# Attention scores on all 128 rows of TensorE, with mask and maximum in one VectorE instruction

## The chip, the cores and the metric

The kernel runs on one core of one Trainium2 chip. The metric is device time in microseconds (us) of one execution, as the median of several timed runs; lower is better. Beside the timed runs there is one profiled execution, from which every row below comes. A core has TensorE (PE in the profile; its weight loads are listed apart as PEld), VectorE (DVE), ScalarE (ACT), GpSimd (POOL) and SyncE (SP), which start transfers and work side by side and wait for each other by semaphores. SBUF is the on-chip memory with 128 partitions; PSUM is the small memory in 8 banks into which TensorE writes.

## The reference

Two layers over 256 positions of width 1024. A layer is a feed-forward part, a mixer, a second feed-forward part and a gated addition. The mixer holds a sparse attention of 8 query heads over 2 key heads (64 numbers each) and a gated delta rule of 4 heads. The change is in the attention:

```python
def masked_softmax(s, mask):
    s = jnp.where(mask, s.astype(jnp.float32), NEG_INF)
    return jnp.where(mask, jax.nn.softmax(s, axis=-1), 0.0)
...
        s_c = jnp.einsum('bqhgd,bnhd->bhgqn', qb, k_cmp)
        p_cmp = masked_softmax(s_c, cmp_end[None, :] <= t[:, None])
        o_cmp = jnp.einsum('bhgqn,bnhd->bqhgd', p_cmp.astype(v_cmp.dtype), v_cmp)
...
        s_s = jnp.einsum('bqhgd,bhqnld->bhgqnl', qb, k_sel).reshape(
            b, NSA_KV_HEADS, NSA_GROUP, Q_BLOCK, n_sel * SLC_BLOCK)
        p_s = masked_softmax(s_s, m_s).reshape(b, NSA_KV_HEADS, NSA_GROUP, Q_BLOCK, n_sel, SLC_BLOCK)
        o_slc = jnp.einsum('bhgqnl,bhqnld->bqhgd', p_s.astype(v_sel.dtype), v_sel)
...
        s_w = jnp.einsum('bqhgd,bkhd->bhgqk', qb, kwb)
        p_w = masked_softmax(s_w, m_w)
        o_win = jnp.einsum('bhgqk,bkhd->bqhgd', p_w.astype(vwb.dtype), vwb)
        return gb[..., 0:1] * o_cmp + gb[..., 1:2] * o_slc + gb[..., 2:3] * o_win
```

There are three branches: over 15 compressed keys, over selected blocks of 64 keys, and over a window of 512. With 256 positions there are only 4 blocks and 16 may be selected, and no position lies outside the window, so the second and the third branch are plain causal attention, each with its own keys and values.

## The kernel before

**Tiling.** Positions stand in two tiles t of 128. Weights come from HBM through SP's queue in units of 128x2048 numbers (raw) and are split into a rounded part hi by ScalarE (L158) and a remainder lo by VectorE (L159). Every large product is three matmuls, hi by hi, hi by lo and lo by hi, so that it is nearly as exact as fp32. L273 is the helper through which all matmuls go and L277 the one for transposes, so that groups of these lines are told apart by the tiles they name: bA is the PSUM pool of the projections, bG that of the delta rule, bN that of the attention (4 banks).

**Order.** A mixer is seven generators (queries, keys, values and gates of the delta rule, the attention, the projections of weights, the output projection). The function weave resumes in a fixed ranking whichever is due; each yield says how long its result will take, and a running count of PE time sets what is due. This gives the order in which instructions are written; a scheduler then sets the order on each engine by priority and by when tiles of the pools (TAGS gives the number of buffers, BANKS the PSUM banks) come free. On an engine instructions run in that order.

**The attention.** rope (L625, L626) rotates: two products and an addition, of which GpSimd does the product with the sine and VectorE the others. nsa_prepare transposes the rotated tile into a bank and splits it into hi and lo, for the keys and for the queries. A tile then has the numbers of key head 0 on partitions 0 to 63 and those of key head 1 on 64 to 127, and all queries of four heads beside each other. compressed makes the scores over the compressed keys: one matmul writes the mask into the bank (identity by mask), then 12 of 32 columns add the scores. softmax(t, a) does the other two branches for tile t and half a of the heads. For each key head it takes a bank of 512 columns; one matmul writes the causal mask, and three matmuls per query head on 64 rows add the scores of both branches; the two key heads' matmuls alternate, on different halves of the rows. VectorE then takes the maximum of each query's row from PSUM (L1023, one instruction for 4 rows of 128 or 2 of 256), multiplies it by -1/8 (L1024), and ScalarE takes the exponent out of PSUM into SBUF tiles p, with the sum (L1027). values transposes p (L277, bN<-first,p; first holds the identity) and multiplies by the values (bN<-pT,kv). tile 0 has one pass of softmax per half, tile 1 two.

**What runs beside it.** gdn_inverse inverts the triangular matrices of the delta rule by levels (tiles ad, ab, T and TT; L816 multiplies by a level's mask on GpSimd, L832 and L836 update T and TT on VectorE). conv (L714) is the causal convolution on VectorE, gdn_scan the recurrence over 4 chunks (vb,TT is the first product of a chunk).

## Time and profile before

| what | value |
|---|---|
| median of 3 timed runs | 1193.28 us (1193.14 to 1193.42) |
| the profiled execution's own time | 1193.65 us |
| its span | 1191.9 us |
| PE busy | 1160.6 us, 97% |
| VectorE busy | 737.6 us, 62% |
| ScalarE busy | 644.4 us, 54% |
| GpSimd busy | 96.9 us, 8% |

The span runs from the first to the last instruction of the profiled execution; 1.75 us of its time lie around that. Busy time is the time in which an engine had an instruction in work. The share is a mean over the whole kernel, most of which is dense projections; the two mixers' attention lies at 240 to 364 us and at 827 to 951 us.

### The profile page before, as it was taken

To read this page: it belongs to the slowest core of one execution; us is meant where nothing else is said; L and a number is where in the kernel's file an instruction comes from. 1 tells how busy PE (TensorE), PEld (TensorE's weight loads), DVE (VectorE), ACT (ScalarE), POOL (GpSimd) and SP (SyncE) were. 2 spreads that over 40 slices of the span, in tenths; PEclk is the share of its full clock that TensorE was granted. 3 is DMA by queue.
4 is the path that set the end of the run, shared out by engine and by line. 5 is a ranking of instruction groups with operands and counts; after the bars stand their busy time and mean duration, and the time that the engine had idled before them with its cause. 6 is when DMAs were issued, how large, how long until landed. Compare 5 with 4: busy or idle time off the path is not lost.

```text
span 1191.9 us, 16067 instructions
## 1 busy us (share of the span) xinstructions
PE 1160.6 (97%) x6222; PEld 933.9 (78%) x6222; DVE 737.6 (62%) x1191; ACT 644.4 (54%) x1157; POOL 96.9 (8%) x137
## 2 busy tenths in 40 slices
PE   8999999989999999999999999999899999999996
PEld 6888888867767788888878888888676778888885
DVE  5656546887846655554675564479779365565454
ACT  7544536735766544534665454466358565454463
POOL 0000000270100000000000000004501000000011
PEclk9999999999999999999999999999999999999999
DMA  8545653422213545464554565553223144555540
GB/s 313 183 172 214 244 190 133 179 105 76 102 37 141 186 167 212 164 211 164 177 206 153 206 250 198 188 178 112 104 74 104 37 171 159 201 186 201 205 177 36
DMA packets 29292, 194.15 MB, mean 163 GB/s; under 512 B 3232, under 2 KB 3616, under 8 KB 7200
## 3 DMA queue, kind: packets, MB, share of 16 engines
q1 hardware_dynamic: 28496, 191.56, 45.0%
q10 hardware_dynamic: 720, 1.57, 0.3%
q8 instruction: 49, 0.80, 0.3%
q14 instruction: 27, 0.22, 0.1%
HBM read 192.07 MB, written 1.05 MB: 162 GB/s over the span
## 4 chain that ended last, share of the span: by engine, by line
PE 90%; DVE 4%; ACT 3%; issue 2%; POOL 1%; DMA 0%; POOLq 0%; SPq 0%; ACTq 0%; DVEq 0%
PE bA L273 50%; PE bN L273 31%; PE bG L277 4%; PE bG L273 4%; DVE lo L159 2%; PE bN L277 1%; ACT hi L158 1%; ACT p L1027 1%; POOL mn L625 0%; DMA x<-x 0%; ACT junk L925 0%; DVE mx L1023 0%; DVE ad L786 0%; DVE mn L626 0%; DVE g L450 0%
## 5 line engine op out<-in xcount | busy, mean ns | idle before, releaser
L273 PE MATMUL bA<-hi,xT 128*128 128x512 f32 (+1 forms) x1856 | 601.2, 397 | 0.9 <-DVE xT L327 0.5
L159 DVE TENSOR_TENSOR lo<-raw,hi 128x1024 fp32r<-128x1024 f32 (+2 forms) x358 | 436.8, 1225 | 213.1 <-ACT hi L158 190.7
L158 ACT ACTIVATE hi<-raw 128x1024 fp32r<-128x1024 f32 (+2 forms) x358 | 373.4, 1048 | 224.0 <-PE bN L273 118.1
L273 PEld LDWEIGHTS bA<-hi,xT 128*128 128x128 f32 x1856 | 345.3, 189 | 74.6 <-issue 4.5
L273 PE MATMUL bA<-lo,xT 128*128 128x512 f32 (+1 forms) x928 | 360.7, 390 | 0.0
L273 PEld LDWEIGHTS bA<-lo,xT 128*128 128x128 f32 x928 | 175.4, 189 | 33.9 <-issue 0.7
L273 PE MATMUL bN<-hi,n 128*128 128x512 f32 x480 | 154.2, 393 | 0.0
L273 PE MATMUL bN<-hi,g 128*128 128x512 f32 x448 | 139.9, 391 | 0.0
L273 PEld LDWEIGHTS bN<-hi,n 128*128 128x128 f32 x480 | 90.2, 188 | 18.4 <-issue 0.3
L273 PEld LDWEIGHTS bN<-hi,g 128*128 128x128 f32 x448 | 83.8, 188 | 17.1
L273 PE MATMUL bN<-lo,n 128*128 128x512 f32 x240 | 94.9, 396 | 0.0
L389 DVE SCALAR_TENSOR_TENSOR m<-bA,r,m 128x256 f32<-128x256 f32 x88 | 42.1, 479 | 79.6 <-ACT m L387 79.6
L273 PE MATMUL bN<-lo,g 128*128 128x512 f32 x224 | 87.8, 392 | 0.0
L387 ACT ACTIVATE m<-bA,r 128x256 f32<-128x256 f32 x88 | 41.5, 471 | 72.9 <-PE bA L273 69.7
L298 POOL TENSOR_SCALAR r<-ss 128x1 f32<-128x1 f32 x18 | 6.0, 333 | 827.3 <-ACT junk L291 827.3
L273 PEld LDWEIGHTS bN<-lo,n 128*128 128x128 f32 x240 | 45.1, 188 | 8.6
L273 PEld LDWEIGHTS bN<-lo,g 128*128 128x128 f32 x224 | 42.1, 188 | 8.5
L327 DVE SCALAR_TENSOR_TENSOR xT<-bG,first,xT 128x128 fp32r<-128x128 f32 x96 | 31.7, 346 | 25.5 <-ACT xT L326 25.4
L326 ACT ACTIVATE xT<-bG,first 128x128 fp32r<-128x128 f32 x96 | 32.9, 362 | 16.5 <-DVE xT L327 15.8
L395 ACT ACTIVATE g<-bG 128x256 fp32r<-128x256 f32 x48 | 18.0, 376 | 42.4 <-PE bG L277 42.2
L277 PEld LDWEIGHTS bG<-first,m 128*128 128x128 f32 x192 | 25.9, 140 | 16.9 <-DVE m L931 3.3
L277 PE MATMUL bG<-first,m 128*128 128x128 f32 x192 | 37.2, 274 | 1.8 <-DVE m L931 1.6
(219 smaller groups left out, 954.2 us busy)
## 6 DMA issues: line engine op xcount, KB each, us to landing
raw<-up SPq DMA_DIRECT2D x86, 1024.0 KB, 4.9
raw<-dn SPq DMA_DIRECT2D x44, 1024.0 KB, 4.9
raw<-win SPq DMA_DIRECT2D x24, 1024.0 KB, 4.8
raw<-wout SPq DMA_DIRECT2D x8, 1024.0 KB, 4.8
raw<-gate SPq DMA_DIRECT2D x8, 1024.0 KB, 4.8
cw<-cw SPq DMA_DIRECT2D x8, 512.0 KB, 8.1
raw<-up SPq DMA_DIRECT2D x4, 512.0 KB, 7.0
raw<-proj SPq DMA_DIRECT2D x2, 1024.0 KB, 4.7
```

Of the source, the lines that this page charges most:

```text
L158: nc.scalar.activation(hi[:, s:f], raw[:, a + s:a + f], AF.Copy)
L159: nc.vector.tensor_tensor(lo[:, s:f], raw[:, a + s:a + f], hi[:, s:f].bitcast(F32), op=OP.subtract)
L273: self.nc.tensor.matmul(out, lhsT, rhs, start=start, stop=stop, skip_group_check=part)
L277: self.nc.tensor.transpose(out, x, self.ident[:n, :n])
L298: nc.gpsimd.tensor_scalar(r, self.ss[:, 0:1], self.ss[:, 1:2], EPS, op0=OP.add, op1=OP.add)
L326: nc.scalar.activation(hi[h][:, i, cs], b[:, i, :], AF.Copy, scale=g)
L327: nc.vector.scalar_tensor_tensor(lo[h][:, i, cs], b[:, i, :], g, hi[h][:, i, cs].bitcast(F32), op0=OP.mult, op1=OP.subtract)
L387: nc.scalar.activation(s, bs[t][:, :256], AF.Silu, scale=r[t])
L389: nc.vector.scalar_tensor_tensor(h, bs[t][:, 256:], r[t], s, op0=OP.mult, op1=OP.mult)
L395: nc.scalar.activation(hh[c // 2][o], b, AF.Copy)
L1027: nc.scalar.activation(p[kv][:, i + j, br], sc[kv][:, j, br], AF.Exp, scale=0.125, bias=m[:, i + j, br:br + 1], accum_out=sm[kv][:, i + j, ...
```

## The change

The two parts of a query, hi and lo, are stacked on the partitions, and the keys are doubled so that they stand on both halves. A product over 128 rows with the keys' hi then gives hi by hi plus lo by hi, and one with the keys' lo gives hi by lo plus lo by lo: two matmuls in place of three. For key head 0 the query's hi is on partitions 0 to 63 and its lo on 64 to 127; for key head 1 the other way round, since after the transpose its numbers stand on the upper half.

- rope, called with twice, writes each rotated key twice beside itself; nsa_keys transposes 128 columns per key head and branch, four transposes per tile in place of two, and splits 128x512 numbers in place of 128x256.
- nsa_queries makes for each tile t a tile nq of 4 heads x 2 key heads x 128; hi and lo of each key head are written by two instructions of ScalarE and two of VectorE on 64 partitions.
- In compressed the mask matmul goes; 8 matmuls of 32 columns (hi beside lo) take the place of 12, and VectorE adds mask, lo part and hi part in two instructions. The small key matmul of compress becomes one in place of two, its weights stand twice in the packed constants (w2), and two GpSimd fills go.
- In softmax the mask matmuls go. VectorE's tensor_tensor_reduce adds the mask (from the packed constants, now 256 wide: zeros, then the triangle), writes the masked scores to p in SBUF and their maximum to mx, in one call for each row of 128 or 256. In the order of instructions each call is two, "ISA p,mx" and "ISA mx". ScalarE's exponent now reads and writes p in SBUF.
- The pool n has 9 buffers in place of 8, the pool n2 (2 buffers) is gone; the ple part's two tiles move from n2 to mn. Three casts of identity and masks at the start go.

```diff
@@ rope
-    def rope(self, z, t, nh):
+    def rope(self, z, t, nh, twice=False):
...
+        if twice:
+            w = self.tile("mn", [128, nh, 2, 64])
+            nc.vector.tensor_tensor(w, *(a[:, :, None, :].to_broadcast([128, nh, 2, 64]) for a in (o, u)), op=OP.add)
+            return w
         nc.vector.tensor_tensor(o, o, u, op=OP.add)
         return o
@@ compress
-        for kv in range(2):
-            self.mm(kb[kv * 64:kv * 64 + 64], w2[0], hT[:, 0, kv, :NCMP])
+        self.mm(kb, w2[0], hT[:, 0])
...
-        for p in range(2):
-            nc.gpsimd.memset(kcm[p].rearrange("p a n -> p (a n)").bitcast(F32), 0.0)
-        for kv, R in enumerate(self.HALF):
-            hi, lo = (p[R, kv, :NCMP] for p in kcm)
-            nc.vector.tensor_copy(hi, kb[R])
-            nc.vector.tensor_tensor(lo, kb[R], hi.bitcast(F32), op=OP.subtract)
+        nc.vector.tensor_copy(kcm[:, :, 0], kb)
+        nc.vector.tensor_tensor(kcm[:, :, 1], kb, kcm[:, :, 0].bitcast(F32), op=OP.subtract)
@@ in place of nsa_prepare
+    def nsa_keys(self, g, z):
...
+        hi, lo = (self.tile("n", [128, 2, 2, S], F32R) for _ in range(2))
+        for t in range(NT):
+            src = self.rope(z(t).rearrange("p (h d) -> p h d", h=4), t, 4, True)
+            yield 2.0
...
+            b = self.bank("N", [128, 2, 2, 128])
+            for br in range(2):
+                for kv in range(2):
+                    h = 2 * br + kv
+                    self.tr(b[:, kv, br], src[:, h].rearrange("p a d -> p (a d)"))
+            ts = slice(t * 128, (t + 1) * 128)
+            nc.scalar.activation(hi[:, :, :, ts], b, AF.Copy)
+            nc.vector.tensor_tensor(lo[:, :, :, ts], b, hi[:, :, :, ts].bitcast(F32), op=OP.subtract)
...
+    def nsa_queries(self, g, z):
...
+            q = self.tile("n", [128, 4, 2, 128], F32R, name="nq")
+            for kv, (R, O) in enumerate(((A, B), (B, A))):
+                nc.scalar.activation(q[R, :, kv], b[R], AF.Copy)
+                nc.vector.tensor_tensor(q[O, :, kv], b[R], q[R, :, kv].bitcast(F32), op=OP.subtract)
@@ compressed
-            cs = self.bank("N", [128, 4, 2, 16])
-            self.mm(cs.rearrange("p i k n -> p (i k) n"), self.idr, self.maskc[:, t, None, :].to_broadcast([128, 8, 16]), True, False, True)
+            cs = self.bank("N", [128, 4, 2, 2, 16])
             for i in range(4):
-                scores(cs[:, i], t, slice(0, 128), i, lambda b: kcm[b])
+                for kv in range(2):
+                    self.mm(cs[:, i, kv], q[t][:, i, kv], kcm[:, kv])
...
+            nc.vector.tensor_tensor(pf, cs[:, :, 1], self.c[:, None, C_CM + t * 16:C_CM + t * 16 + 16]
+                                    .to_broadcast([128, 8, 16]), op=OP.add)
+            nc.vector.tensor_tensor(pf, cs[:, :, 0], pf, op=OP.add)
@@ softmax
-                    self.mm(sc[kv][:, :, :, t * 128:t * 128 + 128].rearrange("p j b k -> p (j b) k"), self.idr,
-                            self.mask[:, None, :].to_broadcast([128, 2 * nb, 128]), True, False, True)
-                for j in range(nb):
-                    for n, (x, y) in enumerate(((0, 0), (0, 1), (1, 0))):
-                        for kv, R in enumerate(HALF):
-                            self.mm(sc[kv][:, j], q[x][R, a * 2 + i + j, cols(t)], k[y][R, :, :nk * 128],
-                                    False, n == 2, True)
-                for kv in range(2):
+                    for j in range(nb):
+                        for part in range(2):
+                            self.mm(sc[kv][:, j], q[t][:, a * 2 + i + j, kv], k[part][:, kv, :, :nk * 128],
+                                    not part, bool(part), True)
                     m = mx[kv]
-                    nc.vector.tensor_reduce(m[:, s], sc[kv], axis=AX.X, op=OP.max)
+                    for j in range(nb):
+                        for br in range(2):
+                            nc.vector.tensor_tensor_reduce(p[kv][:, i + j, br], sc[kv][:, j, br],
+                                                           self.c[:, C_TRI + 128 - t * 128:C_TRI + 256], 1.0, -3e38,
+                                                           op0=OP.add, op1=OP.max,
+                                                           accum_out=m[:, i + j, br:br + 1])
...
-                            nc.scalar.activation(p[kv][:, i + j, br], sc[kv][:, j, br], AF.Exp, scale=0.125,
+                            nc.scalar.activation(p[kv][:, i + j, br], p[kv][:, i + j, br], AF.Exp, scale=0.125,
```

The change also moves instructions, in three places that matter. The first is GpSimd's order in the first mixer where the queries are rotated: L625 (L619 after) is rope's product with the sine for the keys (kv) and the queries (q), L816 (L809 after) the level masks of the triangular inverse. Before:

```order
L795 TENSOR_TENSOR ke<-y,eg 128x512
L816 TENSOR_TENSOR ab<-ad,cst 128x256 x5
L625 TENSOR_TENSOR mn<-q,cst 128x8x32 x2
L816 TENSOR_TENSOR ab<-ad,cst 128x256 x2
L625 TENSOR_TENSOR mn<-q,cst 128x8x32 x2
L816 TENSOR_TENSOR ab<-ad,cst 128x256 x5
```

After:

```order
L788 TENSOR_TENSOR ke<-y,eg 128x512
L809 TENSOR_TENSOR ab<-ad,cst 128x256 x7
L619 TENSOR_TENSOR mn<-q,cst 128x8x32 x2
L809 TENSOR_TENSOR ab<-ad,cst 128x256
L619 TENSOR_TENSOR mn<-q,cst 128x8x32 x2
L809 TENSOR_TENSOR ab<-ad,cst 128x256 x4
```

Seven level masks stand ahead of the first half of the queries now, and five did before.

The second is VectorE's order in the first mixer at tile 0's compressed scores (tiles pc, m and s) and first softmax. Before:

```order
L981 TENSOR_REDUCE m_2508<-bN 128x8
L982 TENSOR_TENSOR pc<-bN,m_2508 128x128
L985 TENSOR_REDUCE s_2512<-pc 128x8
L986 RECIPROCAL s_2512<-s_2512 128x8
L987 SCALAR_TENSOR_TENSOR s_2512<-s_2512,cst,sg 128x8
L989 TENSOR_TENSOR pc<-pc,s_2512 128x128
L1023 TENSOR_REDUCE mx<-bN 128x4 x2
L1024 TENSOR_SCALAR mx<-mx 128x4 x2
```

After:

```order
L990 TENSOR_TENSOR pc<-bN,cst 128x128
L826 STREAM_TRANSPOSE TT<-T 128x256
L992 TENSOR_TENSOR pc<-bN,pc 128x128
L1034 ISA p,mx<-bN,cst 128x128
L1034 ISA mx 128x1
L994 TENSOR_REDUCE m_2500<-pc 128x8
L1034 ISA p,mx<-bN,cst 128x128
L1034 ISA mx 128x1
L995 TENSOR_TENSOR pc<-pc,m_2500 128x128
L1034 ISA p,mx<-bN,cst 128x128
L1034 ISA mx 128x1
```

In place of two reductions stand eight pairs, each with a row of its own, and the compressed scores' chain is spread between them.

The third is PE's order in the first mixer where the last values of tile 1 meet the scan of the delta rule. Before:

```order
L277 MATMUL bN<-first,p 128x128 x4
L277 MATMUL bG<-first,y 128x128 x2
L273 MATMUL bG<-vb,TT 64x128 x2
L277 MATMUL bN<-first,p 128x128 x4
L273 MATMUL bG<-vb,TT 64x128 x2
L277 MATMUL bN<-first,p 128x128 x3
L273 MATMUL bN<-pT,kv 64x256 x4
L277 MATMUL bN<-first,p 128x128
L273 MATMUL bG<-y,ao 64x128 x4
L277 MATMUL bN<-first,p 128x128 x7
```

After:

```order
L271 MATMUL bG<-first,y 128x128 x2
L267 MATMUL bN<-pT,kv 64x256 x3
L271 MATMUL bN<-first,p 128x128 x5
L271 MATMUL bG<-first,y 128x128 x4
L271 MATMUL bN<-first,p 128x128
L267 MATMUL bG<-vb,TT 64x128 x4
L271 MATMUL bN<-first,p 128x128 x4
L267 MATMUL bG<-y,ao 64x128 x4
```

Before, the scan's first product (bG<-vb,TT) stands among the first transposes of tile 1's weights; now most of these transposes and of their products with the values stand ahead of it.

## Rows read from the trace of the kernel before

**Rows 1.** The page: its head, part 1 (busy time), part 4 (chain).

```profile
span 1191.9 us, 16067 instructions
...
PE 1160.6 (97%) x6222; PEld 933.9 (78%) x6222; DVE 737.6 (62%) x1191; ACT 644.4 (54%) x1157; POOL 96.9 (8%) x137
...
PE 90%; DVE 4%; ACT 3%; issue 2%; POOL 1%; DMA 0%; POOLq 0%; SPq 0%; ACTq 0%; DVEq 0%
```

**Rows 2.** Windows: us, busy PE, PEld, DVE, ACT, POOL; clock; DMA; GB/s.

```profile
240.40:266.90 26.50, 21.70 (x205) 17.26 (x203) 22.18 (x38) 9.42 (x15) 19.86 (x20) 0.94 0.26 97
266.90:290.20 23.30, 23.23 (x290) 18.50 (x290) 16.23 (x40) 11.51 (x32) 2.92 (x3) 1.00 0.25 93
290.20:331.90 41.70, 40.24 (x221) 29.69 (x220) 35.96 (x87) 30.72 (x89) 3.70 (x6) 1.00 0.25 87
331.90:363.50 31.60, 30.44 (x196) 21.94 (x195) 14.16 (x36) 17.39 (x44) 2.43 (x4) 1.00 0.09 30
```

**Rows 3.** Chain of waits: start, length in us, what; pieces on TensorE.

```profile
140.22 49.44 PE bN L273 x218
...
275.77 1.55 PE bN L273 x13
...
290.83 0.44 PE bN L277 x4
...
296.99 0.58 PE bN L273 x4
298.00 1.13 PE bN L273 x8
...
303.43 1.01 PE bN L273 x4
...
329.99 1.29 PE bN L273 x4
```

**Rows 4.** Timeline of TensorE: start, length, instructions, [idle before them].

```profile
260.11 1.15 PE L273 MATMUL bG<-T,ab 64*64 64x64 f32 x32 [2.53 <-DVE T L832]
...
277.96 0.63 PE L273 MATMUL bN<-mask,idr 128*128 128x512 f32 x2
278.52 0.97 PE L273 MATMUL bN<-n,n 64*128 64x256 f32 x12
279.43 1.15 PE L273 MATMUL bG<-T,ab 64*64 64x64 f32 x32
```

**Rows 5.** Timeline of VectorE, same columns.

```profile
242.31 1.25 DVE L626 TENSOR_TENSOR mn<-mn 128x256 f32<-128x256 f32 x1
...
256.43 1.21 DVE L626 TENSOR_TENSOR mn<-mn 128x512 f32<-128x512 f32 x1 [1.31 <-POOL mn L625]
...
259.56 0.74 DVE L832 TENSOR_TENSOR T<-T,bG 128x256 f32<-128x256 f32 x2
...
280.11 1.28 DVE L1023 TENSOR_REDUCE mx<-bN 128x4 f32<-128x512 f32 x2
...
296.06 2.03 DVE L714 SCALAR_TENSOR_TENSOR y<-bG,small,y 128x255 f32<-128x255 f32 x5
```

**Rows 6.** Single lines: shortest/median/longest in ns, first and last start, forms.

```profile
L775 DVE SCALAR_TENSOR_TENSOR dc<-bG,gc,cst x16: 339/339/342, 237.2 to 827.3; 128x128 f32<-128x128 f32 x16
...
L714 DVE SCALAR_TENSOR_TENSOR y<-bG,small,y x72: 465/474/483, 212.9 to 913.8; 128x255 f32<-128x255 f32 x24, 128x254 f32<-128x254 f32 x24, 128x253 f32<-128x253 f32 x24
```

**Rows 7.** Timeline of ScalarE: an exponent with its accumulator read.

```profile
281.76 0.19 ACT L1027 ACTIVATION_READ_ACCUMULATOR p<-bN,mx 128x1 f32 x1
281.86 0.36 ACT L1027 ACTIVATE p<-bN,mx 128x128 f32<-128x128 f32 x1
```

**Rows 8.** Timeline of GpSimd at the queries' rotation.

```profile
254.01 2.39 POOL L625 TENSOR_TENSOR mn<-q,cst 128x256 f32<-128x256 f32 x2
256.36 1.87 POOL L816 TENSOR_TENSOR ab<-ad,cst 128x256 f32<-128x256 f32 x2
```

**Rows 9.** Windows again, two microseconds after the idle stretch; columns as above.

```profile
262.00:264.00 2.00, 2.00 (x11) 1.16 (x11) 0.70 (x1) 0.00 (x0) 1.29 (x2) 0.50 0.00 0
```

More of the change, by code (lines that the diff above doesn't have):

```diff
@@ L72, in constants @@
     c[:, C_SIN:C_SIN + 128] = sin.reshape(2, 128, 64).transpose(1, 0, 2).reshape(128, 128)
-    c[:, C_TRI:C_TRI + 128] = np.where(q <= r, 0.0, NEG)
+    c[:, C_TRI + 128:C_TRI + 256] = np.where(q <= r, 0.0, NEG)
     for t in range(NT):
@@ L236, in constants @@
         nc.gpsimd.memset(self.half, 0.5)
-        self.idr = self.cp.tile([128, 128], F32R, name="idr")
-        nc.gpsimd.tensor_copy(self.idr, self.ident)
-        self.mask = self.cp.tile([128, 128], F32R, name="mask")
-        nc.gpsimd.tensor_copy(self.mask, self.c[:, C_TRI:C_TRI + 128])
-        self.maskc = self.cp.tile([128, NT, 16], F32R, name="maskc")
-        nc.gpsimd.tensor_copy(self.maskc.rearrange("p t n -> p (t n)"), self.c[:, C_CM:C_CM + 32])
     def units(self, stages):
@@ L405, in ple @@
         nc.scalar.dma_start(praw, self.a["pT"][l].rearrange("p (k t) -> p k t", k=2))
-        ph, pl = self.tile("n2", [128, 2, S], F32R), self.tile("n2", [128, 2, S], F32R)
+        ph, pl = self.tile("mn", [128, 2, S], F32R), self.tile("mn", [128, 2, S], F32R)
         nc.scalar.activation(ph, praw, AF.Copy)
@@ L548, in attention @@
             yield from until(z, "kv", 1.0)
-            yield from self.nsa_prepare(g, "nk", lambda t: z["kv"][:, t, :256], 4, "n2")
+            yield from self.nsa_keys(g, lambda t: z["kv"][:, t, :256])
             yield from until(z, "q", 1.0)
-            yield from self.nsa_prepare(g, "nq", lambda t: z["q"][:, t], 8, "n")
+            yield from self.nsa_queries(g, lambda t: z["q"][:, t])
             yield from self.nsa(g, z["kv"])
@@ L634, in compress @@
         vc = [head(t, 160) for t in range(NT)]
-        kcm = [self.tp.tile([128, 2, 16], F32R, tag=f"kcm{i}", bufs=1, name=f"kcm{i}") for i in range(2)]
+        kcm = self.tp.tile([128, 2, 2, 16], F32R, tag="kcm", bufs=1, name="kcm")
         vcm = self.tp.tile([128, 8, 64], F32, tag="vcm", bufs=1, name="vcm")
@@ L672, in compress @@
         yield 0.6
-        w2 = [self.sm[:, l, S_W2 + 64 * i:S_W2 + 64 * i + 64] for i in range(2)]
-        kb = self.bank("N", [128, NCMP])
+        w2 = self.sm[:, l, S_W2:S_W2 + 128], self.sm[:, l, S_W2 + 128:S_W2 + 192]
+        kb = self.bank("N", [128, 2, 16])
         vb = self.bank("N", [128, 64])
-        for kv in range(2):
-            self.mm(kb[kv * 64:kv * 64 + 64], w2[0], hT[:, 0, kv, :NCMP])
+        self.mm(kb, w2[0], hT[:, 0])
         hv = self.tile("mn", [128, 4, 2, 16])
@@ L942, in gdn_finish @@
         g["gdn"] = get
[L944 removed]
+    def nsa_keys(self, g, z):
         nc = self.nc
[L947 to L948 removed]
+        hi, lo = (self.tile("n", [128, 2, 2, S], F32R) for _ in range(2))
         for t in range(NT):
[L950 removed]
+            src = self.rope(z(t).rearrange("p (h d) -> p h d", h=4), t, 4, True)
             yield 2.0
[L952 to L958 removed]
+            b = self.bank("N", [128, 2, 2, 128])
[6 more added lines that the diff above has]
+            nc.vector.tensor_tensor(lo[:, :, :, ts], b, hi[:, :, :, ts].bitcast(F32), op=OP.subtract)
+        g["nk"] = hi, lo
+        yield 1.0
+    def nsa_queries(self, g, z):
+        nc = self.nc
+        A, B = self.HALF
+        g["nq"] = []
+        for t in range(NT):
+            src = self.rope(z(t).rearrange("p (h d) -> p h d", h=8), t, 8)
+            yield 2.0
+            b = self.bank("N", [128, 4, 128])
+            for f in range(4):
+                self.tr(b[:, f], src[:, 2 * f:2 * f + 2].rearrange("p h d -> p (h d)"))
+            q = self.tile("n", [128, 4, 2, 128], F32R, name="nq")
+            for kv, (R, O) in enumerate(((A, B), (B, A))):
+                nc.scalar.activation(q[R, :, kv], b[R], AF.Copy)
+                nc.vector.tensor_tensor(q[O, :, kv], b[R], q[R, :, kv].bitcast(F32), op=OP.subtract)
+            g["nq"].append(q)
         yield 1.0
@@ L1006, in softmax @@
             nb = 2 // nk
-            ps[t, a] = p = [self.tile("n", [128, 2, 2, nk * 128], name="p") for _ in HALF]
+            p = [self.tile("n", [128, nb, 2, 2, nk * 128], name="p") for _ in range(nk)]
+            ps[t, a] = p = [p[kv][:, 0] if t else p[0][:, kv] for kv in range(2)]
             mx, sm = ([self.tp.tile([128, 2, 2], F32, tag=n, bufs=4, name=n) for _ in HALF] for n in ("mx", "smx"))
```

28 lines of the change are left out of this document (8 added, 20 removed).

## The prediction

> **What bounds the kernel now.** I read the page first, then busy time by stretch, then the chain of waits, then the timelines of single engines. The page gives a span of 1191.9 us with TensorE busy for 97% of it and VectorE for 62%, and the chain that ended last runs over TensorE for 90% [rows 1]. So a matmul taken away should count, unless the place it is taken from waits for something else. The change lies in the two mixers alone, and their attention occupies 123 us of each. The table by stretch [rows 2] cuts these 123 us into four, and a different thing limits each. In the first (keys and queries rotated, the triangular inverse begun) TensorE is busy for 21.7 of 26.5 us and VectorE for 22.2: PE waits. In the second (inverse, first scores) PE is full, 23.2 of 23.3, and VectorE has 7.1 us to spare. In the third (the other scores, the convolutions of q and v) PE is busy for 40.2 of 41.7 and VectorE for 36.0: two engines near full at once. In the fourth (the scan, values, start of the output projection) PE is busy for 30.4 of 31.6 and VectorE for only 14.2. The second mixer runs the same program some 587 us later, so I work out one mixer and double it.
>
> **The change, part by part.** All durations are from the profiled execution of 1193.65 us, which is 0.37 us above the median of the three timed runs.
>
> TensorE, compressed scores: a mask matmul and 12 score matmuls of 32 columns take 1.55 us [rows 3]. That is about 0.11 us for a matmul of 32 columns, as much as a 128-column transpose takes (four in 0.44 [rows 3]), so a narrow one costs its weight load. Eight remain: 0.9 us. Twice per mixer: -1.2.
>
> TensorE, first tile: two mask matmuls and 12 of 256 columns run from 277.96 to the next group's start at 279.43, 1.47 us [rows 4]. Eight matmuls of 256 columns on 128 rows replace them. A 512-column matmul on 128 rows takes 0.227 us (218 of them in 49.44 us [rows 3]), so half the columns are 0.114 and the eight 0.91. Twice: -1.1.
>
> TensorE, second tile: four iterations. Where both heads' banks were free, masks and three pairs took 1.13 us together [rows 3]. Where they were not, each head ran by itself, in 1.01 to 1.29 [rows 3], as long as the pair. Two iterations went the first way (one of them cut by a transpose group; I take it as equal) and two the second: 2 x 1.13 + 4 x 1.1 = 6.7 us. After: 16 x 0.227 = 3.6. -3.0.
>
> TensorE, keys: four transposes more at 0.11, +0.4; one small matmul of the compression less, -0.1. Sum for TensorE: -5.0 us per mixer, -10 in all, if nothing else ended later.
>
> VectorE, maximum: a 128x512 maximum steps at 0.60 us (two in 1.28 less the tail [rows 5]), 12 per mixer, 7.2 us. In their place stand 16 instructions of 128 elements, 16 of 256, and behind each a read of its accumulator; the trace has neither. The nearest rows for the first are a two-tensor instruction from PSUM with a scalar pointer: 0.339 us for 128 elements and 0.474 for 255 [rows 6]; five of the latter back to back take 2.03 [rows 5], a step of 0.39, so 0.26 for the short one. For the read, ScalarE's accumulator read is nearest: 0.19 us long, with the next instruction 0.10 after it began [rows 7]. I take 0.10, so pairs of 0.36 and 0.49: 13.6 us, +6.4. The ends are 0.20 and 0.33 with nothing for the read (+1.3, no scalar to fetch, by the ratio of 0.60 for 512) and full durations with a full read, 0.53 and 0.66 (+11.8).
>
> VectorE, other: two more operations of about 0.25 per compressed tile, +1.0; four half-height subtractions for the queries instead of two full ones, which cost as much each, +1.3; keys twice as wide, +0.3 each for two subtractions and two rotations, +1.2. ScalarE gets two query copies more and reads scores from SBUF; the third stretch has it at 30.7 of 41.7 [rows 2], so I charge nothing, and at most the 1.2 us of the copies if that cover went. Removed fills and casts on GpSimd lie in the first microsecond or in idle time: nothing.
>
> Now by stretch.
>
> First: +1.7. GpSimd's order moves: two multiplications by level masks, which now stood behind the rotation of the queries' first half, come ahead of it. The two took 1.87 us, the rotation before them 2.39 [rows 8]. VectorE's addition for these queries already waited 1.31 us for GpSimd at 256.43 [rows 5], and behind it in VectorE's queue stand a key subtraction, a weight subtraction and the update T at 259.56, for which PE sat idle 2.53 us [rows 4, 5]. Add 0.9 for the wider keys ahead, take off 0.2 that the weights gain from a quiet GpSimd: T comes about 2.6 late. PE gets three more projection matmuls into that gap (0.7), and does fewer later while its clock is at half (granted 0.50 in 262 to 264 [rows 9]), so I give back 0.9. The ends: +0.8 if only the wider keys count, +4 if PE idles long enough that the clock falls a second time.
>
> [...]
>
> Second: -1.7, TensorE's 0.6 and 1.1. VectorE gains 1.3 (queries), 0.5 and 16 x 0.36 - 4 x 0.60 = 3.4, 5.2 us, under its 7.1 idle [rows 2].
>
> Third: +0.5. PE loses 3.6 (0.6 and 3.0), but VectorE gains 16 x 0.49 - 8 x 0.60 + 0.5 = 3.5 against 5.7 idle, and PE must take in work from the fourth stretch: the chain of conv, maximum and exponent then ends on VectorE, slightly later.
>
> Fourth: -2.0. In PE's order 18 transposes and 8 value matmuls of the second tile now stand ahead of the scan's first product. At 0.11 and 0.29 (two in 0.58 [rows 3]) they are 4.3 us; about half should come out of the stretch, the rest was cover for the scan's hops between engines.
>
> Sum: +1.7 - 1.7 + 0.5 - 2.0 = -1.5 per mixer, -3.0 in all: 1193.65 - 3.0 = 1190.65, and 0.37 less as a median, **1190.3 us**.
>
> **The rivals.** (1) TensorE's whole saving arrives: 2 x 5.0 less, 1183.3. For it: 90% of the chain. Against: the first stretch, where PE waits, and the third, where VectorE is at 86%. (2) VectorE becomes the bound of stretches two and three, slower: pairs at 0.53 and 0.66. The third gains 16 x 0.17 = 2.7 and the second, with 7.9 against 7.1 idle, 1.4, so the mixer is at +2.6 and the run at 1198.5. It decides from about 0.06 us more per pair than I took, where the gain is used up. For it: two accumulators' worth of instructions that no row prices, in a queue that projection weights share. Against: VectorE waits for exponents at the first tile now. (3) The first stretch costs +3.2, since PE's clock falls again after the longer wait: everything cancels, 1193.3. (4) Pairs of 64-row matmuls already fill the array, and stacking buys nothing but the masks: first tile -0.2 each, second tile 0 (3 x 0.227 + 2 x 0.114 = 0.91 before, 0.91 after). Then the first stretch is +1.7, the second -1.0, the third +0.5 and the fourth -1.0 (less room on PE): +0.2 per mixer, and the run at 1193.65 + 0.4 - 0.37 = 1193.7. Against it: pairs broken at half the iterations, where a head alone took as long as two.
>
> [...]
>
> **How the numbers follow.** Forecast 0.45, whole saving 0.10, VectorE bound 0.27, clock 0.10, pairs 0.08. A difference under 0.2% (2.4 us: 1190.9 to 1195.7) is about what a measurement of this kernel can't tell from none. The forecast's own range is 1187 to 1193 (the cheap end of the accumulator below, half of the fourth stretch's gain lost above), and I put two thirds of it under 1190.9. Faster: 0.30 of the forecast and the whole saving, 0.40. Slower: the VectorE case and half of the clock case, 0.32. Between: 0.15 of the forecast, the pairs and the other half of the clock case, 0.28. Since cases of both signs hold much, the whole range has to reach past 1198.5 above and near the whole saving below: 1184 to 1200.
>
> **What would show it.** The score matmuls' groups at 0.23 us per 512 columns with no head running alone; the accumulator read's step on VectorE; VectorE's addition for the queries waiting longer for GpSimd and PE idle near 260 for 3 to 4 us; VectorE near 95% in the third stretch; a fourth stretch under 30 us. It is wrong if pairs cost over 0.55 us, or if PE idles in the third stretch waiting for weights or maxima.

## The result and the profile after

The changed kernel takes **1181.8 us** as a median of four runs (1180.72 to 1182.93) against 1193.35 for the kernel before in the same comparison: a ratio of 0.9899, with a 95% interval of 0.9881 to 0.9916. It is faster by 11.55 us. The forecast was 1190.3, with a range of 1184 to 1200: the sign was right, the size was a quarter of what came, and the time lies below the range. The four runs fall in two groups, 1180.7 and 1181.3 us with a mean granted clock of 0.998, and 1182.3 and 1182.9 with 0.994.

The profiled execution took 1180.72 us. Its page answers to [rows 1]: TensorE is as full as before, and VectorE has barely more to do (742.2 us, 737.6 before).

```profile
span 1178.9 us, 16017 instructions
...
PE 1146.9 (97%) x6150; PEld 929.2 (79%) x6150; DVE 742.2 (63%) x1303; ACT 646.9 (55%) x1161; POOL 95.9 (8%) x130
...
PE 89%; DVE 3%; ACT 3%; issue 2%; POOL 2%; DMA 0%; POOLq 0%; SPq 0%; ACTq 0%
```

The four stretches of the first mixer. They are cut at the same instructions as [rows 2] (the key casts, the fourth product with T, the first transposes of gq, the transposes just ahead of the scan), but the fourth ends here at the first matmul that reads g (bN<-hi,g), 3 us behind the end in [rows 2]. Columns: length in us, busy time of PE, PEld, DVE, ACT, POOL, then granted clock, DMA share, GB/s.

```profile
240.27:264.87 24.60, 19.95 (x205) 16.05 (x204) 19.67 (x34) 9.53 (x15) 18.82 (x20) 1.00 0.28 102
264.87:286.70 21.83, 21.72 (x277) 18.32 (x278) 19.26 (x66) 13.07 (x34) 3.85 (x3) 1.00 0.24 81
286.70:330.60 43.90, 41.92 (x235) 31.35 (x234) 39.39 (x133) 35.60 (x101) 3.45 (x4) 1.00 0.29 106
330.60:359.97 29.37, 28.22 (x173) 21.30 (x172) 13.55 (x28) 13.82 (x32) 2.51 (x4) 1.00 0.10 36
```

The fourth in the kernel before, to the same matmul:

```profile
331.90:366.37 34.47, 33.31 (x208) 24.28 (x207) 14.98 (x38) 19.14 (x46) 2.43 (x4) 1.00 0.13 48
```

First 26.5 to 24.6, second 23.3 to 21.8, third 41.7 to 43.9, fourth 34.5 to 29.4: 6.3 us less for the mixer. The third stretch is longer because it takes in work that the fourth no longer has (235 recorded PE instructions in place of 221, and 173 in place of 208 in the fourth). Counted by dense matmuls (the products of hi and lo parts in projections and feed-forward, 4272 on record in either kernel), the piece from the 900th to the 1300th, which holds the first mixer, takes 171.3 us in place of 177.6, and the piece from the 3000th to the 3400th, with the second mixer, 168.4 in place of 174.6: 6.3 and 6.2 us less.

Now the terms. On TensorE, the first tile's eight score matmuls, and two of the second tile's (the step is from one start to the next):

```profile
275.35 1.10 PE L267 MATMUL bN<-n,nq 128*128 128x256 f32 x8
276.38 1.15 PE L267 MATMUL bG<-T,ab 64*64 64x64 f32 x32
...
292.40 0.62 PE L267 MATMUL bN<-n,nq 128*128 128x512 f32 x2
292.86 0.39 PE L267 MATMUL bA<-hi,xT 128*128 128x512 f32 x1
```

Eight in 1.03 us (0.91 was taken), two in 0.46, so 0.23 each, as taken.

On VectorE, the new pairs for 128 elements, and one for 256 between convolutions:

```profile
286.00 0.28 DVE L1034 CUSTOM_DVE_ANT_0 p<-bN,cst 128x128 f32<-128x128 f32 x1
286.21 0.08 DVE L1034 DVE_READ_ACCUMULATOR2_ANT mx<- 128x1 f32 x1
286.21 0.29 DVE L1034 CUSTOM_DVE_ANT_0 p<-bN,cst 128x128 f32<-128x128 f32 x1
...
316.10 0.42 DVE L1034 CUSTOM_DVE_ANT_0 p<-bN,cst 128x256 f32<-128x256 f32 x1
316.44 0.08 DVE L1034 DVE_READ_ACCUMULATOR2_ANT mx<- 128x1 f32 x1
316.44 0.48 DVE L707 SCALAR_TENSOR_TENSOR y<-bG,small,y 128x254 f32<-128x254 f32 x1
```

The next instruction starts when the accumulator read starts, so the read costs nothing: a pair steps at **0.21 us** for 128 elements and **0.34** for 256, where the forecast had taken 0.36 and 0.49. That is 16 x 0.21 + 16 x 0.34 = 8.8 us per mixer in place of 13.6.

In the first stretch: GpSimd's product with the sine for the queries, VectorE's addition that waits for it, a weight subtraction, the update T, and TensorE behind it. These answer to [rows 4, 5, 8].

```profile
255.38 1.42 POOL L619 TENSOR_TENSOR mn<-q,cst 128x256 f32<-128x256 f32 x2
```

```profile
256.84 0.69 DVE L624 TENSOR_TENSOR mn<-mn 128x512 f32<-128x512 f32 x1 [2.02 <-POOL mn L619]
...
258.05 1.22 DVE L159 TENSOR_TENSOR lo<-raw,hi 128x1024 fp32r<-128x1024 f32 x1
259.18 0.74 DVE L825 TENSOR_TENSOR T<-T,bG 128x256 f32<-128x256 f32 x2
```

```profile
259.74 1.15 PE L267 MATMUL bG<-T,ab 64*64 64x64 f32 x32 [2.45 <-DVE T L825]
```

The addition waits 2.02 us for GpSimd where it had waited 1.31, as foreseen. But T is not late: from the key casts to T it is 18.9 us, and before it was 19.1.

### The profile page after: what moved, and what is told of

Same layout as the page of the kernel before. It is cut to its first block, busy times and chain, and to the rows that moved or that the text cites. A ratio compares the mean times of both kernels' runs of the same rounds, so it can differ in the third digit from the quotient of the medians.

```text
span 1178.9 us, 16017 instructions
## 1 busy us (share of the span) xinstructions
PE 1146.9 (97%) x6150; PEld 929.2 (79%) x6150; DVE 742.2 (63%) x1303; ACT 646.9 (55%) x1161; POOL 95.9 (8%) x130
## 3 DMA queue, kind: packets, MB, share of 16 engines
q1 hardware_dynamic: 28496, 191.69, 44.6%
## 4 chain that ended last, share of the span: by engine, by line
PE 89%; DVE 3%; ACT 3%; issue 2%; POOL 2%; DMA 0%; POOLq 0%; SPq 0%; ACTq 0%
PE bA L267 49%; PE bN L267 31%; PE bG L271 4%; PE bG L267 4%; ACT hi L158 1%; PE bN L271 1%; DVE lo L159 1%; POOL mn L619 1%; POOL ab L809 1%; DMA x<-x 0%; ACT junk L918 0%; ACT p L1041 0%; ACT junk L734 0%; DVE ad L779 0%; DVE y L707 0%
## 5 line engine op out<-in xcount | busy, mean ns | idle before, releaser
L267 PE MATMUL bN<-hi,n 128*128 128x512 f32 x448 | 143.6, 392 | 0.0
L267 PEld LDWEIGHTS bN<-hi,n 128*128 128x128 f32 x448 | 84.0, 188 | 16.8 <-issue 0.3
L267 PE MATMUL bN<-lo,n 128*128 128x512 f32 x224 | 89.1, 398 | 0.0
L267 PEld LDWEIGHTS bN<-lo,n 128*128 128x128 f32 x224 | 42.1, 188 | 8.6 <-issue 0.8
```

What stands on the lines that cost most here:

```text
L267: self.nc.tensor.matmul(out, lhsT, rhs, start=start, stop=stop, skip_group_check=part)
```

## The experiments

All medians stand beside 1193.2 to 1193.8 for the kernel before in the same comparisons, and 1181.8 for the changed kernel. The "third stretch" is here from the first transposes of gq to the scan's first product, first and second mixer; the last column is the piece between the third and the fourth product with T, in which the granted clock was 0.75 in both mixers of before, 0.72 in the first of e1_stack and 1.00 in both of the changed kernel.

| kernel | median, us | third stretch | third to fourth T |
|---|---|---|---|
| before | 1193.35 | 42.4 / 42.4 | 6.8 / 6.9 |
| changed | 1181.8 | 44.6 / 44.6 | 5.1 / 5.1 |
| e1_stack | 1183.55 | 44.5 / 44.5 | 6.1 / 5.1 |
| e2_ttr | 1189.6 | 43.9 / 43.9 | 5.3 / 6.8 |
| e3_vec2 | 1199.36 | 51.0 / 52.3 | 6.1 / 5.1 |
| e4_rope_dve | 1177.98 | 46.0 / 45.8 | 6.2 / 6.2 |
| e5_vec_half | 1191.47 | 50.2 / 50.3 | 6.1 / 6.1 |
| e6_vec_t0 | 1185.6 | 45.7 / 47.7 | 5.1 / 6.1 |
| e7_noneg | 1178.36 | 42.8 / 42.8 | 5.1 / 5.1 |
| e8_both | 1173.93 | 42.8 / 42.8 | 6.2 / 6.2 |
| e9_offchain | 1186.74 | 48.9 / 47.8 | 5.1 / 5.1 |
| e10_before_rope | 1188.27 | 42.4 / 42.4 | 5.3 / 5.3 |
| e11_pool | 1181.92 | 43.4 / 43.4 | 6.2 / 6.2 |

**Which half of the change gives the gain.** e1_stack keeps the stacked scores and takes mask and maximum as before:

```diff
+                    self.mm(sc[kv][:, :, :, t * 128:t * 128 + 128].rearrange("p j b k -> p (j b) k"), self.idr,
+                            self.mask[:, None, :].to_broadcast([128, 2 * nb, 128]), True, False, True)
...
-                            nc.vector.tensor_tensor_reduce(p[kv][:, i + j, br], sc[kv][:, j, br],
...
+                    nc.vector.tensor_reduce(m[:, s], sc[kv], axis=AX.X, op=OP.max)
```

> The changed kernel with the causal masks as matmuls and the maximum as one reduction again, and the exponent out of PSUM; scores stay stacked on 128 rows, the compressed scores as changed. Theory A (the time follows TensorE's work, whatever VectorE does): the 12 mask matmuls per mixer come back, 4 of 512 columns at 0.227 us and 8 of 256 at 0.114, 1.8 us per mixer, so 1181.8 + 3.6 = 1185.4 us. Theory B (pairs of 64-row matmuls filled the array already, and the masks were the gain): stacking alone keeps little more than the compressed scores' 1.2 per mixer, 1193.3 - 2.4 = 1191 us.

Measured 1183.55 us (ratio 0.9917, 0.9892 to 0.9942). Theory B falls: stacking with the compressed scores alone brings nearly 10 of the 11.5 us (in the profiled executions some 2.5 of them stand in the last column of the table, which is the clock; more on it below). The masks cost 1.75 us, half of what A expects from TensorE. The maximum as one reduction is 7.2 us of VectorE per mixer against 8.8 for the pairs, and TensorE idles less for it in the third stretch (44.40 - 42.76 = 1.6 us against 2.4).

e2_ttr is the other half: the 64-row scores of before, mask and maximum on VectorE.

```diff
-                    self.mm(sc[kv][:, :, :, t * 128:t * 128 + 128].rearrange("p j b k -> p (j b) k"), self.idr,
-                            self.mask[:, None, :].to_broadcast([128, 2 * nb, 128]), True, False, True)
...
-                    nc.vector.tensor_reduce(m[:, s], sc[kv], axis=AX.X, op=OP.max)
+                            nc.vector.tensor_tensor_reduce(p[kv][:, i + j, br], sc[kv][:, j, br],
```

> The kernel before, its scores on 64 rows as they were, with the mask added and the maximum taken by VectorE and the exponent from SBUF; compressed scores as before. Theory A with pairs that stay broken at half of the iterations: only the mask matmuls go, 1193.3 - 3.6 = 1189.7 us. Theory C (a PSUM bank comes free when VectorE has read it and no longer waits for four exponents, so both heads run together): the second tile's four iterations take 3 x 0.227 = 0.68 us each in place of 6.7 in all, -4.0, and the first tile loses 1.0, so 5 us per mixer and 1183.3 us: nearly the whole gain without any stacking.

Measured 1189.6 us (ratio 0.9961, 0.9946 to 0.9976), theory A to the tenth; C falls, the pairs stay broken. That it fits to the tenth is in part luck: in the profiled executions 1.6 of the 4.2 us stand in the last column (6.8 / 6.9 to 5.3 / 6.8), and A knows nothing of the clock. The timeline of TensorE in e2_ttr shows both kinds (start, length; six matmuls are both heads, three one head):

```profile
300.34 0.96 PE L271 MATMUL bN<-n,n 64*128 64x512 f32 x3
...
318.98 0.96 PE L271 MATMUL bN<-n,n 64*128 64x512 f32 x6
319.87 0.50 PE L271 MATMUL bA<-hi,xT 128*128 128x512 f32 x1
```

Six matmuls of both heads take as long as three of one. The six take 0.89 us to the next group, and four stacked ones 4 x 0.23 = 0.92. So the rival on pairs had its fact right and its conclusion wrong: a full pair is as good as stacking, but in the first pass over tile 1 all four heads ran alone. Stacked, the two matmuls of one head by itself step at 0.23 us each (at 292.40 us above), so that a head needs no other beside it. Which wait keeps the banks apart was not tried.

**What VectorE's price is worth.** e3_vec2 gives every pair twice, e5_vec_half those of key head 0 (range(2 - kv)), e6_vec_t0 those of tile 0 (range(2 - t)).

```diff
+                            for _ in range(2):
                                 nc.vector.tensor_tensor_reduce(p[kv][:, i + j, br], sc[kv][:, j, br],
```

> The changed kernel with each mask-and-maximum instruction given twice, the second with the same result. A pair steps at 0.21 us for 128 elements and about 0.29 for 256 in the trace, so VectorE has 8 us more per mixer: 3.4 in the stretch of the first scores, where it is idle for 2.6 of 21.8 us, and 4.6 in the stretch after it, where it is idle for 4.5 of 44.6. Theory A (VectorE has room, the prediction's price was simply too dear): 0.5 to 2 us per mixer, 1183 to 1186 us. Theory D (VectorE is as near to being the bound as the prediction had it, and was only cheaper than thought): the pairs now cost 0.42 and 0.58, between the forecast's price and that of its VectorE rival, and the gain is gone: 1190 to 1194 us.

Measured 1199.36 us (ratio 1.0046, 1.0024 to 1.0067): slower than the kernel before, past both theories. The expectation had read 0.29 us for 256 elements, and the step is 0.34: VectorE has 8.8 us more per mixer, and 8.8 us per mixer is what it costs.

> The changed kernel with the mask-and-maximum instructions of key head 0 given twice and those of key head 1 once. A pair steps at 0.21 us for 128 elements and 0.34 for 256, so VectorE has 4.4 us more per mixer and 13.2 for all pairs: the price that the prediction took for the changed kernel (13.6). Theory D1 (in these stretches VectorE's time arrives in the end one for one, as twice the price cost 17.5 us for 17.6 us of work): 1181.8 + 8.8 = 1190.6 us, so that the prediction's error was the price and nothing else. Theory D2 (there is room first, as the idle shares say, 2.6 and 4.5 us per mixer, and only what goes beyond it costs): 1182 to 1185 us, and at its own price the prediction would still have been too slow.

Measured 1191.47 us (ratio 0.998, 0.9961 to 0.9999), as D1 has it. At the price that the prediction took for the pairs, the kernel lands 1.2 us from its forecast. In the profiled executions about 2 of the 9.7 us stand in the last column (5.1 to 6.1 in both mixers), ahead of a mixer's first pair.

> The changed kernel with the mask-and-maximum instructions given twice for tile 0 alone, 16 x 0.21 = 3.4 us more per mixer, nearly all in the stretch of the first scores. If VectorE counts everywhere one for one: 1181.8 + 6.7 = 1188.5 us. If it counts in the third stretch alone (in the run with all of them twice TensorE stood still at 318 to 332 us, in the third stretch): 1182 to 1184 us.

Measured 1185.6 us (ratio 0.9936, 0.9912 to 0.996), between the two. So "one for one" is not a law here, and the traces say what it is made of. First the third stretch of the changed kernel (first mixer), then of e5_vec_half, then of e6_vec_t0 in its first and second mixer, columns as above:

```profile
286.70:331.30 44.60, 42.19 (x236) 31.39 (x234) 40.09 (x135) 35.60 (x101) 3.45 (x4) 1.00 0.29 104
```

```profile
286.50:336.70 50.20, 46.21 (x239) 33.17 (x237) 44.18 (x161) 35.63 (x101) 3.45 (x4) 0.90 0.27 94
```

```profile
286.50:332.20 45.70, 41.89 (x238) 31.24 (x236) 41.96 (x156) 36.51 (x106) 3.45 (x4) 1.00 0.29 104
868.80:916.50 47.70, 44.38 (x239) 32.75 (x237) 42.06 (x156) 36.67 (x106) 3.45 (x4) 0.93 0.27 99
```

In e5_vec_half the stretch is 5.6 us longer. TensorE's idle time accounts for 1.6 of it (3.99 in place of 2.41); the other 4.0 is the same work at a lower granted clock, 0.90 in place of 1.00. In e6_vec_t0 the same code ran once at 1.00 and once at 0.93, and the second took 2.0 us longer. What TensorE did before the clock fell in e5_vec_half (timeline of TensorE, then windows of 2 us):

```profile
323.03 0.63 PE L271 MATMUL bN<-first,p 128*128 128x128 f32 x4 [1.47 <-DVE mx L1035]
324.74 0.79 PE L267 MATMUL bN<-pT,kv 128*64 128x256 f32 x4 [1.08 <-ACT pT L1061]
```

```profile
322.00:324.00 2.00, 0.63 (x4) 0.42 (x4) 2.00 (x7) 2.00 (x5) 0.00 (x0) 1.00 0.51 78
324.00:326.00 2.00, 1.26 (x7) 0.75 (x8) 1.99 (x8) 2.00 (x8) 0.00 (x0) 0.78 0.92 385
326.00:328.00 2.00, 1.31 (x5) 0.46 (x3) 1.78 (x7) 1.26 (x3) 0.00 (x0) 0.50 0.15 61
328.00:330.00 2.00, 2.00 (x6) 0.61 (x5) 2.00 (x9) 0.00 (x0) 0.00 (x0) 0.50 0.00 0
```

VectorE is full, the last maxima of tile 1 come late, TensorE has run out of dense work to put in between, waits 1.47 and 1.08 us in a row, and then runs at a granted clock of 0.50 until about 335 us (0.50 from 326 to 334, 0.66 from 334 to 336, 1.00 behind it). In the changed kernel the same place has one wait of 1.73 us for pT, and the clock stays at 1.00. In e4_rope_dve (below) it has one of 1.74, and there the clock fell: 46.0 us in place of 44.6. First the changed kernel, then e4_rope_dve:

```profile
324.01 0.65 PE L267 MATMUL bN<-pT,kv 128*64 128x256 f32 x4 [1.73 <-ACT pT L1060]
```

```profile
321.41 0.65 PE L267 MATMUL bN<-pT,kv 128*64 128x256 f32 x4 [1.74 <-ACT pT L1060]
284.10:330.10 46.00, 43.71 (x236) 32.04 (x234) 40.04 (x135) 35.66 (x101) 3.45 (x4) 0.96 0.28 101
```

So a later maximum makes TensorE wait, and whether the clock falls behind such a wait is not settled by its length here.

e9_offchain puts about the same amount of work beside the chain:

```diff
                         nc.vector.tensor_scalar(p[kv][:, i, br], p[kv][:, i, br], m[:, i, br:br + 1], None, op0=OP.mult)
+                        if not kv:
+                            nc.vector.tensor_reduce(self.tiny(1, "jk"), p[kv][:, i, br], axis=AX.X, op=OP.max)
```

> The changed kernel with as much extra VectorE work as the run with key head 0's instructions twice, but off the attention's chain: after each scaling of p for key head 0 a maximum of the scaled row into a scrap tile that nobody reads (128 or 256 elements, about 0.2 and 0.35 us each, 4.4 us per mixer). Theory G (VectorE's queue as such is short, whoever's work is in it): about 1190 us, as with the work in the chain (1191.5). Theory H (it is the chain from scores over maximum and exponent to the freed bank that grows longer; work beside it finds room): 1182 to 1185 us.

Measured 1186.74 us (ratio 0.9941, 0.9922 to 0.9961), between G and H. Its third stretch is 48.9 us at a clock of 0.90, with 3.3 us idle, 2.74 of them in the wait for pT:

```profile
287.10:336.00 48.90, 45.64 (x237) 33.12 (x234) 43.28 (x145) 35.67 (x101) 3.46 (x4) 0.90 0.28 97
324.95 1.12 PE L267 MATMUL bN<-pT,kv 128*64 128x256 f32 x4 [2.74 <-ACT pT L1062]
```

So work that nobody waits for costs too: conversions and maxima stand behind it in VectorE's order, and of the 4.3 us more in this stretch 0.9 are idle time of TensorE and 3.4 the lower clock. In the chain it costs about twice as much in all (a part of it stands behind the last convolution of the stretch, so that 2.5 us per mixer is rather a lower bound for work beside the chain).

**Less on VectorE.** e7_noneg multiplies the keys by -1/8 where they are split, and the negation of the maximum goes:

```diff
-            nc.scalar.activation(hi[:, :, :, ts], b, AF.Copy)
+            nc.scalar.activation(hi[:, :, :, ts], b, AF.Copy, scale=-0.125)
...
-                                                           op0=OP.add, op1=OP.max,
+                                                           op0=OP.add, op1=OP.min,
...
-                    nc.vector.tensor_scalar(m[:, s], m[:, s], -0.125, None, op0=OP.mult)
```

> The changed kernel with the keys multiplied by -1/8 where they are split, so that VectorE takes a minimum, which is the exponent's bias as it is: the 12 multiplications of the maximum per mixer go (0.08 to 0.16 us each, 1.0 to 1.9 per mixer), and no engine gets an instruction more. Theory D1 (VectorE one for one, in both directions): 2 to 4 us less, 1178 to 1180 us. Theory D2 (there is room on VectorE, so less of it buys nothing): 1181 to 1182 us.

Measured 1178.36 us (ratio 0.987, 0.9842 to 0.9898): D1. The changed kernel's 2.4 us of idle TensorE in the third stretch are gone:

```profile
287.60:330.40 42.80, 42.65 (x237) 31.23 (x235) 38.78 (x115) 33.87 (x93) 3.45 (x4) 1.00 0.28 100
```

That bounds it as well: with 0.15 us left idle, more relief on VectorE has nothing to give in this stretch.

**The first stretch.** e4_rope_dve lets VectorE do the queries' product with the sine; e10_before_rope does the same to the kernel before.

```diff
-            nc.gpsimd.tensor_tensor(u[:, :, h:h + 32], z[:, :, 32 - h:64 - h], tab(C_SIN + h, 32), op=OP.mult)
+            (nc.vector if nh == 8 else nc.gpsimd).tensor_tensor(u[:, :, h:h + 32], z[:, :, 32 - h:64 - h], tab(C_SIN + h, 32), op=OP.mult)
```

> The changed kernel with the queries' products with the sine on VectorE in place of GpSimd (two instructions of 256 elements per tile of positions). Theory E (in the first stretch the update T waits behind an addition that waits 2.0 us for GpSimd, twice, and TensorE idles 4.7 us of 25.5 for that): 1.5 to 2 us per mixer less, about 1178 us. Theory F (VectorE is the chain there, and 1.4 us more work on it comes on top): 1181.8 to 1184 us.

Measured 1177.98 us (ratio 0.9868, 0.9838 to 0.9898): theory E. TensorE's wait before the third product with T, 2.45 us, becomes 0.17 and 0.45:

```profile
256.24 0.68 PE L267 MATMUL bG<-T,ab 64*64 64x64 f32 x16 [0.17 <-DVE T L825]
...
258.04 0.68 PE L267 MATMUL bG<-T,ab 64*64 64x64 f32 x16 [0.45 <-DVE T L825]
```

> The kernel before, with the queries' products with the sine on VectorE in place of GpSimd, as tried on the changed kernel, where it gave 3.8 us. If the change left the first stretch as it was: the same 3.8 here, 1193.3 - 3.8 = 1189.5 us. If the change had made the wait for GpSimd there 1.7 us per mixer longer, as the prediction's sum has it, the kernel before has that much less to gain: 0.4, 1192.9 us.

Measured 1188.27 us (ratio 0.9962, 0.9947 to 0.9976), 5.4 us less than the 1193.7 beside it, more than either expectation. The total doesn't settle it, because in the profiled executions 3 us are the clock (the last column, 6.8 to 5.3 in both mixers). The piece between the second and the third product with T does: VectorE's rotation takes it from 7.4 to 5.8 us in the kernel before, and from 7.9 to 4.9 in the changed one. So the wait for GpSimd did become dearer with the change, by about 1.4 us per mixer of what can be won back, near the prediction's 1.7. But the way up to the second product, from the transposes of gc, became 0.7 us shorter (17.3 to 16.6), so that with the half microsecond more behind it (7.4 to 7.9) the way to T did not grow.

**The clock in the first stretch.** The last column of the table holds the same matmuls in the kernel before, e2_ttr and e10_before_rope (76 to 78 on record): 6.8 us or 5.3. In the versions of the changed kernel it is 6.1 or 5.1 (73 on record). (In e4, e8 and e11 T's order is another.) The windows of e2_ttr, first and second mixer:

```profile
260.40:265.70 5.30, 5.30 (x77) 4.08 (x78) 4.06 (x9) 1.37 (x3) 2.77 (x3) 1.00 0.01 3
844.50:851.30 6.80, 6.80 (x76) 5.16 (x76) 4.07 (x9) 1.34 (x3) 2.78 (x3) 0.75 0.01 4
```

One execution, the same code, the same wait before it (2.40 and 2.41 us): at a granted clock of 0.75 the piece takes 1.5 us more. The profiled execution of before had it in both mixers [rows 9], the changed one in neither. So about 3 of the 13 us between the two profiled executions are this. Whether it strikes after a wait of 2.4 us differs between passes through the same code; after the 0.9 us that e10_before_rope leaves of the wait it struck in neither mixer. Why it strikes in one pass and not in the next stays open.

**Versions that beat both.** e8_both joins e4_rope_dve and e7_noneg.

> The keys' multiplication by -1/8 together with the queries' rotation on VectorE. If both act in their own stretches the gains add: 1178.0 less what the first gives alone, 1175 to 1178 us; if VectorE were one queue over the whole mixer, the rotation's extra work would eat the other's gain, and it stays at 1178 us.

Measured **1173.93 us** (ratio 0.9834, 0.9806 to 0.9861): 7.9 less than the changed kernel, where the two alone give 3.8 and 3.4. They act in different stretches, and their sum is near 7.9. It is not exact, since e4_rope_dve alone loses 1.2 to 1.4 us per mixer in the third stretch (46.0 and 45.8 against 44.6) with the clock's fall after its wait there; e8_both has 42.8 in both mixers, as e7_noneg.

e11_pool takes e8_both and moves half the scaling of p to GpSimd, (nc.gpsimd if kv else nc.vector).tensor_scalar(...).

> The version with keys times -1/8 and the queries' rotation on VectorE, and also the scaling of p by the reciprocal sums for key head 1 on GpSimd, which is idle over the second to fourth stretches: VectorE has about 4 us less per mixer. If VectorE's time counts one for one: 1173.9 - 8 = 1166 us. If GpSimd is slow enough at it that the values come later, or both lock each other out as they did in the first stretch (an addition of 0.69 us took 1.21 beside GpSimd): 1173 to 1178 us.

Measured 1181.92 us (ratio 0.9905, 0.989 to 0.992), 8 us worse than e8_both. The single line shows why (shortest, median, longest in ns), then TensorE's wait in the second mixer, and the scan in the first and the second mixer:

```profile
L1049 DVE TENSOR_SCALAR p<-p,smx x32: 277/316/570, 278.6 to 904.1; 128x128 f32<-128x128 f32 x16, 128x256 f32<-128x256 f32 x16
L1049 POOL TENSOR_SCALAR p<-p,smx x32: 597/918/1658, 279.9 to 906.2; 128x128 f32<-128x128 f32 x16, 128x256 f32<-128x256 f32 x16
```

```profile
906.32 0.55 PE L271 MATMUL bN<-first,p 128*128 128x128 f32 x3 [1.32 <-POOL p L1049]
```

```profile
328.70:347.40 18.70, 18.70 (x127) 13.97 (x127) 5.03 (x11) 7.64 (x18) 2.12 (x3) 1.00 0.00 1
906.80:931.60 24.80, 24.80 (x127) 18.02 (x127) 5.01 (x11) 7.58 (x18) 2.10 (x3) 0.72 0.00 1
```

GpSimd takes 918 ns where VectorE takes 316. The last values wait 1.32 us for it, and in this pass the clock then fell to 0.72 over the scan, which took 24.8 us in place of 18.7 in the first mixer, 6 us in this execution. There was nothing to win: e8_both has TensorE full in the third stretch already (busy for 42.66 of 42.80 us).

## Why the prediction was wrong

**By stretch.** Per mixer the forecast was -1.5 us, and -6.3 came:

| stretch | forecast | measured (first mixer) |
|---|---|---|
| first | +1.7 | -1.9, of it about 1.5 the clock |
| second | -1.7 | -1.5 |
| third | +0.5 | +2.2 |
| fourth | -2.0 | -5.1 |

Two steps failed. The larger is the first stretch: the forecast had the update T 2.6 us late, T came no later than before, and the clock didn't fall; that is 3.6 of the 4.8 us between them. The other is VectorE's price for mask and maximum, taken as 13.6 us per mixer where 8.8 came: the third and fourth stretch together are at -2.9 in place of -1.5, and e5_vec_half, with 13.2, loses most of the gain.

**TensorE's sum, -5.0 per mixer: right.** The matmuls cost what the rows of before said (0.23 per 512 columns, eight compressed ones 0.92 us to the next group; in the kernel before the weight loads of the 12 fill 1.42 us of the matmuls' 1.46, so that a narrow one did cost its weight load), and the two mixers became 6.3 and 6.2 us shorter, of which about 1.5 each is the clock in the first stretch. What is left, about 5, is the sum. The rival "the whole saving arrives" at 1183.3 was nearest to what happened; it was given a chance of 0.10.

**VectorE's price: too dear.** The prediction had no row for an accumulator read behind VectorE and took ScalarE's, 0.10 us of step, and for the main instruction a row with a pointer operand. The read is hidden and the main instruction steps as fast as the shortest bound that was written down (0.20 and 0.33 there, 0.21 and 0.34 here). The value was taken from the middle of the bounds, the truth was the low end. e5_vec_half shows what this was worth: the changed kernel with 13.2 us of pairs per mixer takes 1191.5 us. The trace of the changed kernel has the mask-and-maximum instruction as two, the main one and a read of 0.08 us, 64 of each.

**That e5_vec_half lands on the forecast is partly chance.** The prediction had the third stretch 0.5 us longer at this price, and the first, which holds no pair, 1.7. In e5_vec_half T comes as early as in the changed kernel, and the third stretch is 5.6 us longer than there, 7.8 longer than before. Two terms were wrong in opposite directions.

**First stretch, +1.7: wrong.** The order moved as shown, and VectorE's addition waited 2.02 us in place of 1.31. What was missed is how much shorter instructions become when the two engines no longer run side by side: GpSimd's product 1.42 us in place of 2.39 [rows 8], the addition 0.69 in place of 1.21 [rows 5], the weight subtraction behind it 1.22 in place of 1.74. Two weight subtractions at 244.1 us took 2.88 in place of 3.69 as well, but GpSimd works beside them in both kernels, so that no run shows why. These four are 2.8, enough to cancel the 2.6 up to T. The prediction counted 0.2 us for all this, as what the weights gain from a quiet GpSimd; no run shows that term, and the runs showed 0.52 in its place for the one weight subtraction behind the addition.

**Second stretch, -1.7: right** (23.3 to 21.8). The queries' half-height subtractions cost as much as full ones, as taken: 0.69 us for 64x512 in the changed kernel, and 0.69 for 128x512 before.

**Third and fourth, +0.5 and -2.0: wrong in sum.** Together they came out 2.9 us shorter, not 1.5. (Their 0.29 us for a value matmul is rightly read from [rows 3]: the row's x4 are records, and such a matmul leaves two: 96 on record for 48 in the program.) VectorE's idle share was read as room, 5.7 us in the third stretch, and the extra cost put at a half. It is not room: e9_offchain and e7_noneg show a cost for more and a gain for less while VectorE stands at 90%. The forecast came out near zero in the third because the saving on TensorE was believed to be lost on VectorE, and at the real price most of it was not.

**The rivals.** "VectorE becomes the bound" had the right place and the right sensitivity in direction: at 0.42 and 0.68 per pair (e3_vec2) the kernel is at 1199.4, near that rival's 1198.5 for 0.53 and 0.66. It decides on the price alone, and the price was the thing no row showed. "The clock falls again" named what the traces do show, at the wrong place: in the third stretch it is at 0.90 in e5_vec_half and e9_offchain, where VectorE is late, and in the first it falls in some passes and not in others, with the change (0.72 and 1.00 in the two mixers of e1_stack) and without it (1.00 and 0.75 in e2_ttr). "Pairs fill the array" was refuted by e1_stack.

**The range.** It took the cheap end of the accumulator as 3 us off the forecast and stopped at 1184. Cheap pairs, no loss in the first stretch and a quiet clock together lie below that. The first was written down as an end, the second came out below its end of +0.8, and the third was no term at all; all have the same sign, and the range did not hold them together.

## What to carry to other kernels

When the price of a new instruction decides between two outcomes and no row shows it, its cheap end and its dear end are two forecasts, and the chance belongs on both; the middle is the one value that neither supports. An engine that is busy for 85 to 90% of a stretch and feeds the bottleneck in order may have no room worth the name, as VectorE had none here: test it by doubling the disputed instructions and by taking a small one away. And where an edit moves two engines apart in time, their own durations can change with it (here an addition from 1.21 us to 0.69), so the rows of before price the neighbours and not only the instruction.

## What the runs showed of the hardware that was not expected

- VectorE's accumulator read costs no time behind the instruction that filled it: it is 0.08 us long, and the next instruction starts with it (at 286.21 and at 316.44 us in the changed kernel).
- A short wait of TensorE costs more than itself where the clock falls behind it: in e5_vec_half 1.6 us more idle and 4.0 us more busy time for the same matmuls; in e6_vec_t0 the same stretch took 45.7 us at 1.00 and 47.7 at 0.93 in one execution. A wait of 1.73 us was not followed by a fall, and one of 1.74 in e4_rope_dve was. Within one execution the same piece took 5.3 us at 1.00 and 6.8 at 0.75, in the two mixers of e2_ttr.
- Instructions of GpSimd and VectorE took longer where both engines worked at once: the same two products of GpSimd took 2.39 us in the kernel before (1.71 for the one that VectorE worked beside, 0.72 for the other) and 1.42 with VectorE idle in the changed one; the same addition of VectorE took 1.21 us beside GpSimd and 0.69 alone, a weight subtraction 1.74 and 1.22. It isn't so for every pair: VectorE's product of the queries with the cosine took 0.64 us at 252.81 in the kernel before, beside a level mask of GpSimd, and 1.22 at 253.60 in the changed one, beside level masks as well. No run shows by what the two slow each other.
